# Twelve of sixteen gate projections by seven block products in a pass ahead of the attention, and the attention's fill laid out anew

## The chip, the core and the metric

The kernel runs on one core of one Trainium2 chip. The metric is the device time of one execution in microseconds (us); the kernel before takes 2233.44 us (median of three runs, 2233.07 to 2233.78). All arithmetic is on float32 values. Where the text says that a product is "split", each operand is written as a high part (a cast to the float32r type) plus a low part (the operand minus its high part), and three matmuls stand in place of one: high by high, low by high, high by low.

## The reference

One decoder layer on 1024 tokens of width 1024: a half feed-forward network, two attentions side by side that gates mix, a second half feed-forward network, and a gated embedding. What the change touches is the gate projections, in this middle part:

```python
h = rms_norm(x, mix_norm[i])
fq, fk, fv, f_logit, sq, sk, sv, g_fox, g_sb = split_columns(h @ w_in[i])
log_f = jax.nn.log_sigmoid((f_logit + forget_bias[i]).astype(jnp.float32))
y_fox = forgetting_attention(fq, fk, fv, log_f)      # 8 heads of 64
y_sb = stick_breaking_attention(sq, sk, sv)          # 8 heads of 64
merged = (jax.nn.sigmoid(g_fox) * (y_fox @ w_branch_fox[i])
          + jax.nn.sigmoid(g_sb) * (y_sb @ w_branch_sb[i]))
x = x + merged @ w_out[i]
```

`g_fox` and `g_sb` are 1024 columns each. Together they are 2048 columns of `h @ w_in`, which the kernel makes in sixteen blocks of 128 columns, called gates 0 to 15 here (0 to 7 for fox, 8 to 15 for stick-breaking).

## The kernel before, in words

The layer is worked in this order: the first feed-forward network (`ffn`, with `products` and the loop over `seqn`, then the down projection), the opening of the mixer (`mix_start`, its `end`), the attention with a fill of projections (`attention`), the branch and output projections, the second feed-forward network, and the gated embedding. Within the feed-forward networks the order of all instructions is the order of the code (`tc.manual_schedule`); in the attention the Tile framework places them, with ties set by `order`.

Names that the text uses:

- `hT[half][b]` holds h, transposed (feature by token), for tokens 0 to 511 and 512 to 1023, as high (b = 0) and low (b = 1) part.
- **A plain gate** is made by `g_units` (L901): a weight block of 1024 by 128 is loaded into a RAW buffer (`fetch` or `wload`), `wsplit` makes its high part with a cast on ACT (L136) and its low part with two subtractions on POOL (L146), and for each half of the tokens `feat_steps` (L759) issues 24 matmuls of 128x512 (L763): 3 split terms by 8 blocks of the contraction. The result goes to the array `gd` in HBM, for gates 0 to 7 as it is by a copy on DVE (L914), for gates 8 to 15 after a Sigmoid on ACT (L916). Where gates 0 to 7 are used, `gated` (L1311) loads them and applies the Sigmoid then (L1313).
- **The seven block products** are used in the feed-forward networks alone. A pair of 128-column weight blocks, two halves of the contraction and two halves of the tokens make a 2 by 2 by 2 block product; eight block products are replaced by seven over sums and differences of weight blocks (`sums`, L459, on POOL, and `prep`, L469, which casts on ACT and subtracts on DVE, L112 and L113) and of blocks of h (the `combo_` helpers, L558 to L599, made once). One block product is 12 matmuls of 128x512 (L496). `evict` (L508) joins the products that share a result.
- **The attention** (L1135) goes head by head, h = 0 to 7 fox, 8 to 15 stick-breaking ("sb"). A head has four steps c = 0 to 3, each with two blocks of 128 queries, i = 2c and 2c + 1, against the (i + 1) * 128 keys so far. `scores` (L968) makes the logits on PE (L990, L991) and then works on them: fox on DVE (L995), Exp on ACT (L1001), POOL (L1003); sb with two Sigmoids on ACT (L998, L999), running products on DVE (scans, L966), POOL (L1013, L1017). `apply` (L1027) does the step before: transposes on PE (L1042), a cast on ACT (L1044), a subtraction on DVE (L1045), then the products with v on PE (L1065), summed on ACT and DVE (L1084, L1085).
- **The fill.** In between, `take` (L1244) issues projection matmuls that the attention needs later or that only have to be done somewhere: one twenty-second of what `fill[h]` holds at each of 22 calls in a head, 7 of them in step 0, 4 in step 1, 5 in step 2 and 6 in step 3. `fill[h]` consists of units: half a gate (24 matmuls of 128x512), a quarter of an sb head's q and k projection, or an eighth of a 256-column projection for the fox heads or for v. All sixteen gates were spread over the fill and the stretch ahead of head 0.
- `forget_logs` (L921) and `forget_sums` (L946) make the cumulated forget gates: 27 small operations on DVE with an Exp on ACT, and 30 small matmuls.
- Buffers rotate by tag (`slot`), and PSUM banks by tag (`bank`: "sc" 3, "pt" 2, "av" 1, "pf" 2). An instruction waits until the old use of its buffer is over. SP issues all DMAs, in one queue, in order.

## Time and profile before

| what | before |
|---|---|
| time, median of 3 runs | 2233.44 us (2233.07 to 2233.78) |
| span of the profiled execution | 2230.9 us |
| granted TensorE clock, mean | 1.000 |
| PE busy | 2218.2 us (99%), 10857 matmuls |
| DVE busy | 1490.2 us (67%) |
| ACT busy | 972.1 us (44%) |
| POOL busy | 813.9 us (36%) |
| first attention step (head 0) starts | 725.5 us |
| head 8, the first sb head, starts | 1022.3 us |
| head 15 starts | 1314.8 us |

The span runs from the first to the last instruction of one profiled execution. The runs' list of times does not say which of them was profiled, so the span stands for the execution's own time; it lies 2.5 us under the median of the times. A matmul's end is modelled and matmuls overlap, so PE counts as busy wherever matmuls follow each other closely. The places of the heads come from the first small score matmul of each head. Matmul records match LDWEIGHTS records one to one here.

### The profile page before, as it was taken

How to read it: one execution, taken by the hardware profiler on the slowest of the kernel's cores; microseconds unless marked ns; L12 is line 12 of the kernel's file. 1: busy time of each engine (PE TensorE's matmuls, PEld its weight loads, DVE VectorE, ACT ScalarE, POOL GpSimd, SP SyncE). 2: the span in 40 equal slices, each digit the busy share in tenths (PEclk: the TensorE clock that was granted, in tenths of full speed). 3: DMA queues.
4: the chain of work that ended last, by engine and by line, in shares of the span. 5: the costliest groups of instructions: out<-in, count | busy, mean ns of one | idle time of the engine just before them, and what ended most of it. 6: DMA issues, size and time to landing. Idle time of an engine off the chain costs nothing.

```text
span 2230.9 us, 29212 instructions
## 1 busy us (share of the span) xinstructions
PE 2218.2 (99%) x10857; PEld 1864.3 (84%) x10857; DVE 1490.2 (67%) x2188; ACT 972.1 (44%) x1694; POOL 813.9 (36%) x709
## 2 busy tenths in 40 slices
PE   9999999999999999999999999999999999999999
PEld 7888888888889888888988888887888888888887
DVE  7855545497895565666666676799654555778873
ACT  6433333333454555555456564245333333434441
POOL 0344444310015466455456654400644443200111
PEclk9999999999999999999999999999999999999999
DMA  8232322474433133132124236731423232655132
GB/s 325 94 121 84 112 101 98 152 291 149 147 132 96 29 95 95 29 98 69 39 72 118 62 125 215 266 140 55 140 95 118 85 128 81 254 199 208 62 119 89
DMA packets 187710, 278.03 MB, mean 125 GB/s; under 512 B 27944, under 2 KB 110120, under 8 KB 187568
## 3 DMA queue, kind: packets, MB, share of 16 engines
q1 hardware_dynamic: 187568, 276.17, 36.7%
q8 instruction: 85, 1.39, 0.3%
q14 instruction: 57, 0.47, 0.1%
HBM read 192.47 MB, written 75.27 MB: 120 GB/s over the span
## 4 chain that ended last, share of the span: by engine, by line
PE 91%; DVE 4%; ACT 2%; issue 1%; DMA 1%; POOL 0%; SPq 0%; DVEq 0%; ACTq 0%; POOLq 0%
PE ps L496 36%; PE ps L388 19%; PE ps L763 11%; PE ps L755 7%; PE ps L1307 4%; PE ps L1662 4%; PE ps L1065 3%; PE ps L1042 2%; PE ps L449 2%; PE ps L991 1%; PE ps L990 1%; PE ps L1357 1%; DVE H L113 1%; ACT H L112 1%; ACT T L1001 0%
## 5 line engine op out<-in xcount | busy, mean ns | idle before, releaser
L388 PE MATMUL ps<-H,H 128*128 128x512 f32 x2184 | 497.3, 389 | 0.0
L388 PEld LDWEIGHTS ps<-H,H 128*128 128x128 f32 x2184 | 409.5, 188 | 85.0
L496 PE MATMUL ps<-H,WL 128*128 128x512 f32 x1008 | 238.9, 389 | 0.0
L496 PEld LDWEIGHTS ps<-H,WL 128*128 128x128 f32 x1008 | 189.2, 188 | 39.3
L763 PE MATMUL ps<-H,WH 128*128 128x512 f32 x640 | 176.1, 401 | 0.0
L1045 DVE TENSOR_TENSOR PT<-ps,PT 128x512 fp32r<-128x512 f32 (+1 forms) x160 | 100.6, 634 | 78.5 <-ACT PT L1044 77.6
L496 PE MATMUL ps<-H,Q 128*128 128x512 f32 x576 | 137.4, 389 | 0.0
L396 DVE SCALAR_TENSOR_TENSOR X<-ps,X 128x512 f32<-128x512 f32 x168 | 108.6, 682 | 41.8 <-PE ps L388 41.7
L763 PEld LDWEIGHTS ps<-H,WH 128*128 128x128 f32 x640 | 113.5, 188 | 18.4
L496 PEld LDWEIGHTS ps<-H,Q 128*128 128x128 f32 x576 | 108.1, 188 | 22.5
L1044 ACT CAST PT<-ps 128x512 fp32r<-128x512 f32 (+1 forms) x160 | 86.9, 549 | 85.0 <-PE ps L1042 81.1
L146 POOL TENSOR_TENSOR WL<-RAW,WH 128x512 fp32r<-128x512 f32 (+1 forms) x92 | 108.6, 1202 | 39.4 <-ACT WH L136 28.0
L496 PE MATMUL ps<-X,WL 128*128 128x512 f32 x480 | 115.6, 390 | 0.0
L209 POOL TENSOR_TENSOR PT<-PT,RN 128x1024 f32<-128x1024 f32 x2 | 4.8, 2413 | 295.0 <-ACT RN L203 295.0
L1065 PEld LDWEIGHTS ps<-PT,X 128*128 128x128 f32 x640 | 96.7, 189 | 18.9 <-DVE PT L1045 4.7
L755 PE MATMUL ps<-WH,H 128*128 128x256 f32 (+2 forms) x576 | 111.4, 323 | 0.2 <-DVE log_f L818 0.2
L1065 PE MATMUL ps<-PT,X 128*128 128x256 f32 (+1 forms) x640 | 105.7, 283 | 2.7 <-DVE PT L1045 1.4
L496 PEld LDWEIGHTS ps<-X,WL 128*128 128x128 f32 x480 | 89.9, 188 | 19.1 <-DVE WL L113 0.5
L1003 POOL TENSOR_TENSOR T<-T,l 128x128 f32<-128x128 f32 (+3 forms) x64 | 73.2, 1150 | 88.9 <-DVE l L1002 83.6
L496 PE MATMUL ps<-H,PT 128*128 128x512 f32 x432 | 103.2, 390 | 0.2 <-DVE PT L113 0.2
L283 POOL TENSOR_TENSOR PT<-GF,RN 128x512 f32<-128x512 f32 x20 | 33.2, 1658 | 174.1 <-DVE GF L539 89.9
L496 PEld LDWEIGHTS ps<-H,PT 128*128 128x128 f32 x432 | 80.8, 188 | 18.0 <-DVE PT L113 1.3
(418 smaller groups left out, 4810.8 us busy)
## 6 DMA issues: line engine op xcount, KB each, us to landing
hidden<-PT SPq DMA_DIRECT2D x40, 512.0 KB, 3.1
WH<-in_ffn_w_gate_dram SPq DMA_DIRECT2D x38, 512.0 KB, 5.4
Q<-hidden SPq DMA_DIRECT2D x24, 512.0 KB, 6.4
hidden<-RN SPq DMA_DIRECT2D x22, 512.0 KB, 2.6
KH<-in_ffn_w_up_dram SPq DMA_DIRECT2D x20, 512.0 KB, 6.2
KL<-in_ffn_w_up_dram SPq DMA_DIRECT2D x20, 512.0 KB, 6.9
T<-in_ffn_w_down_dram SPq DMA_DIRECT2D x20, 512.0 KB, 4.4
RAW<-in_w_in_dram SPq DMA_DIRECT2D x18, 512.0 KB, 4.3
```

The lines of the kernel that those rows point to most:

```text
L146: ins = eng_lo.tensor_sub(lo[part], raw[part], f(hi[part]))
L388: pe(nc.tensor.matmul(groups[g][t][:], wt[:, b, k, t * P:(t + 1) * P], act[:, a, k, :], start=(fresh and n == 0), stop=(i in (6, 1, 4) and ...
L396: nc.vector.scalar_tensor_tensor(xs, groups[g][t][:], scale, xs, ALU.mult, ALU.add)
L496: pe(nc.tensor.matmul(ps[:], hl[:, a, k, :], rhs(m, b, k), start=(first and i == 0), stop=(final and i == 11), skip_group_check=True))
L755: pe(nc.tensor.matmul(ps[:, :n], hT[t // 4][a][:, k, (t % 4) * P:(t % 4 + 1) * P], w[k // d][b][:, k % d, :n], start=(i == 0), stop=(i == ...
L763: pe(nc.tensor.matmul(ps[:], w[a][:, k, :], hT[half][b][:, k, :], start=(i == 0), stop=(i == 23)))
L1003: nc.gpsimd.tensor_mul(T[:, :n], T[:, :n], l[:].broadcast_to([P, n]))
L1044: high = nc.scalar.copy(pt[:, 0, :width], ps[:, :width])
L1045: low = nc.vector.tensor_sub(pt[:, 1, :width], ps[:, :width], f(pt[:, 0, :width]))
L1065: pe(nc.tensor.matmul(o, lh, r, start=(kpair == c and i == 0), stop=(kpair == 0 and i == 3)))
L1307: pe(nc.tensor.matmul(ps[:], w[a][:, k, :], yT[g][b][:, k, half * 512:half * 512 + 512], start=(i == 0), stop=(i == 11)))
L1662: pe(nc.tensor.matmul(ps, pl["w"][d, k // 2][b][:, k % 2, m * P:(m + 1) * P], hT[half][a][:, k, cs], start=(i == 0), stop=(i == 23)))
```

## The change

- Gates 0 to 11 leave the fill. `gate_pass`, called at the end of the mixer's opening, makes them in six pairs (`NG = 6`) by seven block products each: 504 matmuls of 128x512 instead of 576. Sums of weight blocks are made on POOL, low parts of weights on DVE; the sums and differences of h are made once, in eighteen DVE operations of 128x1024 (sixteen of them ahead of the first product) and eight ACT casts, from the tiles that the norm left (which are kept: the tags of `last_norms` and `second_half` change).
- The units that were run ahead of the attention (`u1[4:]` and `u2[4:]`, four eighths each of v and of q and k for heads 0 and 1) now run at the start of the pass, between those operations. `forget_logs` comes in the middle of them, `forget_sums` after the thirteenth product.
- The Sigmoid of all gates is applied where they are made; `gated` no longer applies it.
- Gates 12, 13 and 14 stay in the fill of fox heads 2, 4 and 6, and gate 15 in that of heads 12 and 13. `fill` is laid out anew: every head but head 5 holds less, and v for sb heads 12 to 15 is spread over heads 8 to 11.

```diff
+NG = 6
...
-            side = second_half(N[1], (38, 80, 15), lambda: bank("pt"), lambda: bank("pt"), ("PT", "PT", "PT", "Q"))
+            side = second_half(N[1], (38, 80, 15), lambda: bank("pt"), lambda: bank("pt"), ("PT", "PT", "KH", "KH"))
...
+            gate_pass(N)
...
+    def gate_pass(N):
...
+        seqn = [(0, 1), (0, 2), (1, 1), (1, 2), (0, 5), (1, 5), (0, 6), (1, 6), (0, 7), (1, 7), (0, 3), (0, 4), (1, 3), (1, 4), (2, 1), (2, 2), (2, 6), (2, 5), (2, 7)]
...
+        seqn += [(n, 1), (n - 1, 4), (n, 6), (n, 5), (n, 7), (n, 4), (n - 1, 3), (n, 2), (n, 3)]
...
+        def prep(n, m):
+            tag = ("WL", "WL", "WL", "WH", "WH", "WH")[turn_[0] % 6]
...
+            split(hl[:, 0], hl[:, 1], part(n, m), nc.scalar, nc.vector)
+            if m == 1:
+                sums(n)
...
+        def t1(i):
...
+            nc.vector.tensor_sub(c[:], wa(i)[:], c[:])
+            nc.scalar.copy(pair(5, 0, i), c[:])
...
+        def t23(i):
+            nc.vector.tensor_sub(wa(i)[:], wb(i)[:], wa(i)[:])
+            nc.vector.tensor_sub(wb(i)[:], wb(i)[:], C[i][:])
...
+        units = [g for _, g in mx["u1"][4:] + mx["u2"][4:]]
+        load(0)
+        prep(0, 1)
+        t1(0)
+        t1(1)
+        run(units[0])
+        load(1)
+        l1(0)
+        l1(1)
+        run(units[1])
+        prep(0, 2)
+        t23(0)
+        t23(1)
+        run(units[2])
+        prep(1, 1)
+        s(0, 6, wb)
+        run(units[3])
+        mx["sums"] = forget_logs(slot("WH", [P, 6, NT * NH]))
+        s(0, 7, wa)
+        run(units[4])
...
+        run(units[7])
+        s(1, 6, wb)
+        s(1, 7, wa)
+        t4(1)
...
+        for q, (n, m) in enumerate(seqn):
+            evict(n, m, product(n, m))
+            if q == 1:
+                s(0, 4, wa)
+                s(1, 4, wa)
+            for x in seqn[q:q + LA + 1]:
...
+                    prep(*x)
+            if q == 12:
+                forget_sums(mx["sums"])
...
+        fetch(c1w[0], c1w[1])
+        place(c1w[0], c1w[1])
+        fetch(c1w[2])
+        place(c1w[2])
+        fetch(c1w[3])
+        place(c1w[3])
         fs = fst(0)
-        run_all([fs[0], g0[0], fs[1]])
...
+        run_all([fs[0], c1[0], fs[1], c1[1]])
...
+        fill = [c1[2:5], c1[5:], ga + uq[:2], uq[2:], gb + c2[:3], c2[3:], gc, u8]
+        u9, uv = sst(9), v_units(SV + 256, 0, vs1)
+        fill.append(u9 + uv[:2])
+        fill.append(sst(10) + uv[2:4])
+        fill.append(sst(11) + uv[4:6])
+        fill.append(uv[6:] + sst(12))
...
+        fill.append(u + gs_[:n])
+        fill.append(sst(14) + gs_[n:2 * n])
+        fill.append(sst(15) + gs_[2 * n:])
         fox_branch = fox_branch_units()
-        fill.append(g15[1:] + fox_branch[:8])
+        fill.append(fox_branch[:8])
...
         nc.sync.dma_start(dst, gd[gate * KD + m, :, half * 512:half * 512 + 512])
-        order("act", nc.scalar.activation(dst, dst, AF.Sigmoid))
```

How the change moves instructions shows at three places. In each, a row is one instruction of the engine, result `<-` operands, and its width.

DVE at the end of the mixer's opening, first before: after the last statistics of q and k (qkss) come the low part of v (X) and a copy of the forget logits for one unit after the other, each from the bank (ps) that PE has filled.

```order
L849 TENSOR_SCALAR qkss_5018<-qkss_5018 128x16
L113 TENSOR_TENSOR X_4867<-ps_5160,X_4867 128x4x64
L818 COPY log_f<-ps_5160 128x8
L113 TENSOR_TENSOR X_4867<-ps_5188,X_4867 128x4x64
L818 COPY log_f<-ps_5188 128x8
L113 TENSOR_TENSOR X_4867<-ps_5216,X_4867 128x4x64
```

The same place in the changed kernel, where WL is a weight block's split, and Q, PT and KH are blocks of h:

```order
L850 TENSOR_SCALAR qkss_5018<-qkss_5018 128x16
L114 TENSOR_TENSOR WL_5156<-KL_5152,WL_5156 128x512
L1242 TENSOR_TENSOR Q_4760<-PT_4990,Q_4760 128x1024
L1242 TENSOR_TENSOR Q_4763<-PT_5009,Q_4763 128x1024
L114 TENSOR_TENSOR X_4867<-ps_5168,X_4867 128x4x64
L819 COPY log_f<-ps_5168 128x8
L1246 TENSOR_TENSOR X_5163<-Q_4760,X_5163 128x1024
L1246 TENSOR_TENSOR X_5163<-Q_4763,X_5163 128x1024
L114 TENSOR_TENSOR X_4867<-ps_5202,X_4867 128x4x64
L819 COPY log_f<-ps_5202 128x8
L114 TENSOR_TENSOR WL_5230<-KL_5153,WL_5230 128x512
L1249 TENSOR_TENSOR PT_4990<-KH_5037,PT_4990 128x1024
```

Between one unit's two DVE operations and the next unit's now stand two to five operations for the pass.

PE in the last step of head 12 (an sb head), first before: scores of the block of 1024 keys (L990, L991), fill (L763), transposes of the step before (L1042), fill.

```order
L990 MATMUL ps_11025<-KH_10297,Q_10296 128x512
L991 MATMUL ps_11025<-KL_10298,Q_10296 128x512
L990 MATMUL ps_11030<-KH_10297,Q_10296 128x512
L991 MATMUL ps_11030<-KL_10298,Q_10296 128x512
L763 MATMUL ps_10961<-H_4398,WL_10711 128x512 x3
L763 MATMUL ps_11042<-H_4396,WH_10866 128x512 x3
L1042 MATMUL ps_11055<-identf,T_10903 128x128
L1042 MATMUL ps_11055<-identf,T_10927 128x128 x2
L763 MATMUL ps_11042<-H_4396,WH_10866 128x512 x5
```

The same place in the changed kernel:

```order
L991 MATMUL ps_11306<-KH_10784,Q_10783 128x512
L992 MATMUL ps_11306<-KL_10785,Q_10783 128x512
L991 MATMUL ps_11311<-KH_10784,Q_10783 128x512
L992 MATMUL ps_11311<-KL_10785,Q_10783 128x512
L764 MATMUL ps_11255<-H_4397,WH_11030 128x512 x3
L1043 MATMUL ps_11321<-identf,T_11185 128x128
L1043 MATMUL ps_11321<-identf,T_11208 128x128 x2
L764 MATMUL ps_11255<-H_4397,WH_11030 128x512 x4
```

The pieces of fill are 3 and 4 matmuls where they were 6 and 5. Counted over steps 2 and 3 of this head, the fill is 36 matmuls where it was 59.

ACT in head 2 (a fox head), first before: casts of fetched weights (L136), the sum of an output block (L1084), then the Exps of two blocks (L1001) and a cast of transposed weights of the attention (L1044).

```order
L136 CAST WH_6424<-RAW_6327 128x1024
L136 CAST WH_6429<-RAW_6330 128x1024
L1084 COPY Y_5575<-ps_6355 64x256
L1001 ACTIVATE T_6453,l_6455<-T_6453,m_6454 128x384
L1001 ACTIVATE T_6470,l_6472<-T_6470,m_6471 128x512
L1044 CAST PT_6491<-ps_6487 128x384
```

The same place in the changed kernel, where the fill of this head holds gate 12:

```order
L137 CAST WH_7209<-RAW_7089 128x1024
L137 CAST WH_7214<-RAW_7092 128x1024
L1085 COPY Y_6404<-ps_7115 64x256
L917 ACT_TABLE_LOAD
L917 ACTIVATE PT_7206<-ps_7095 128x512
L1002 ACT_TABLE_LOAD
L1002 ACTIVATE T_7193,l_7195<-T_7193,m_7194 128x384
L1002 ACTIVATE T_7223,l_7225<-T_7223,m_7224 128x512
L1045 CAST PT_7243<-ps_7239 128x384
```

A Sigmoid (L917) now stands ahead of the Exps, with a load of ACT's function tables before it and another behind it. Over the whole kernel there are 19 such loads where there were 5; 12 of the added 14 stand in heads 2, 4 and 6.

More of the change, by code (lines that the diff above doesn't have):

```diff
@@ L602, in ffn, with last_norms @@
         nxt = []
[L604 removed]
+        def last_norms(i, t, own, tags_=(("PT", "RN", "GF", "RN"), ("GF", "RN", "KH", "KL"), tail.get("h", ("PT", "PT", "KH", "KL")))):
             if i == 0:
@@ new lines, in attention @@
+        c2[0] = at(c2[0], (place, c2w[3:]))
+        c2[5] = at(c2[5], (fetch, [gcw]))
+        c2[6] = at(c2[6], (place, [gcw]))
+        u8 = sst(8)
+        gc[1] = at(gc[1], (weights, (stacks[8], 1)))
+        fill = [c1[2:5], c1[5:], ga + uq[:2], uq[2:], gb + c2[:3], c2[3:], gc, u8]
[4 more added lines that the diff above has]
+        fill.append(uv[6:] + sst(12))
+        u, gs_ = sst(13), [g_units(m) for m in range(2 * NG + 3, 2 * KD)]
```

180 lines of the change are left out of this document (121 added, 59 removed).

## The prediction

> **What bounds the kernel now.** I read the page first: busy times, then the chain of work that ended last, by engine.
>
> ```profile
> span 2230.9 us, 29212 instructions
> PE 2218.2 (99%) x10857; PEld 1864.3 (84%) x10857; DVE 1490.2 (67%) x2188; ACT 972.1 (44%) x1694; POOL 813.9 (36%) x709
> PE 91%; DVE 4%; ACT 2%; issue 1%; DMA 1%; POOL 0%; SPq 0%; DVEq 0%; ACTq 0%; POOLq 0%
> ```
>
> PE is busy for 99% of the span and carries 91% of the chain. As long as that holds, time goes down only with PE's work. The same chain in order of time has one long piece, in the first feed-forward network, which is made of seven block products:
>
> ```profile
> 62.24 389.12 PE ps L496 x1716
> ```
>
> 389.12 / 1716 = 0.2268 us from one 512-wide matmul to the next, and no wait in 389 us. This is the price of a matmul below. It also shows that the product scheme, with its preparations and evictions, can stay behind PE once it runs.
>
> The 99% are a mean. What the change makes thin is the attention, so I asked for windows: the two halves of an sb head (head 11: steps 0 and 1, then 2 and 3), the second half of head 14, and fox head 6. Columns: window, length, then busy us and instructions of PE, PEld, DVE, ACT, POOL, then PE's clock, DMA share and GB/s.
>
> ```profile
> 1150.50:1170.40 19.90, 19.90 (x109) 16.93 (x109) 9.40 (x18) 9.82 (x21) 7.24 (x11) 1.00 0.19 57
> 1170.40:1191.30 20.90, 20.90 (x114) 17.98 (x114) 17.27 (x21) 13.25 (x28) 15.61 (x16) 1.00 0.34 89
> 1293.50:1314.80 21.30, 20.95 (x113) 17.66 (x112) 17.94 (x23) 15.19 (x31) 12.93 (x16) 1.00 0.42 134
> 952.40:990.40 38.00, 37.31 (x210) 31.40 (x209) 24.80 (x73) 22.27 (x43) 24.42 (x24) 1.00 0.42 112
> ```
>
> In head 11 DVE has 9.40 us of work in the first half and 17.27 in the second, where PE has 20.90. So PE has only 3.6 us more than DVE there: fill is what keeps PE busy while DVE makes the running products and low parts. This is the point on which the change turns.
>
> **What it removes.** 576 matmuls become 504: 72 x 0.2268 = 16.3 us. PE has no idle share to speak of, so all of it would come off the span if nothing else came late. The forget sums move behind the thirteenth product, and with that goes the wait in front of L956:
>
> ```profile
> L956 PE MATMUL ps<-GF,log_f 128*8 128x128 f32 x16 | 3.0, 272 | 1.1 <-DVE log_f L939 1.1
> L956 PEld LDWEIGHTS ps<-GF,log_f 128*8 128x8 f32 x16 | 1.4, 89 | 1.5 <-issue 1.2
> ```
>
> 1.1 us by the matmuls' group, 1.2 by the weight loads'. I take -1.2. What is late there next is the pass's own opening.
>
> **What it adds: the opening of the pass.** Up to the sixth product, PE has the units that it had before (some 23.5 us of the 24.00 in the first row below) and five products of 12 matmuls (60 x 0.2268 = 13.6): 37.1 us. DVE has in that time what it had, and the new blocks of h and of weights. The rows: DVE in the window of before, a 128x1024 subtraction of the same kind in the first network, the low part of a weight block, the old units' own subtraction, and the sum of a bank:
>
> ```profile
> 685.00:709.00 24.00, 24.00 (x202) 23.93 (x200) 10.63 (x30) 8.90 (x19) 16.46 (x12) 1.00 0.26 68
> 685.00:713.00 28.00, 26.94 (x228) 26.28 (x227) 13.61 (x45) 10.14 (x22) 16.99 (x13) 1.00 0.29 76
> L576 DVE TENSOR_TENSOR GF<-Q,GF x2: 1217/1217/1217, 47.8 to 1524.4; 128x1024 f32<-128x1024 f32 x2
> L113 DVE TENSOR_TENSOR WL<-RAW,WL 128x512 fp32r<-128x512 f32 x44 | 41.5, 944 | 11.3 <-ACT WL L112 11.3
> L113 DVE TENSOR_TENSOR X<-ps,X 128x256 fp32r<-128x256 f32 x4 | 1.7, 424 | 9.2 <-ACT X L112 9.2
> L523 DVE TENSOR_TENSOR Y<-Y,ps 128x512 f32<-128x512 f32 x22 | 15.1, 685 | 23.6 <-PE ps L496 23.6
> ```
>
> DVE: 13.6 + 18 x 1.217 = 21.9 + six low parts 5.7 + one sum 0.7 = 41.9 us. DVE's queue is in order, and each projection unit's bank is emptied by an L113 and an L818 that now stand behind two to five of the new operations, so PE waits in small pieces for "ps" and for X, T, GF, and last for the low part of the sixth product. 41.9 - 37.1 = 4.8; I take +5. It is 0 if DVE starts early (ahead of the old units' four subtractions it sat idle for 9.2 us), and 9 if the drains of banks and DVE's total add up rather than overlap.
>
> **The pass once it runs.** A pair is 84 matmuls, 19.05 us of PE. DVE has seven low parts and three sums, 7 x 0.94 + 3 x 0.69 = 8.6 us; the long piece of 389 us above did the same. I cost it at nothing; PE's products hide it, and without that cover it would be up to 8.6 us a pair. The Sigmoids move from the tail to the pass. In the tail they were hidden under PE too, which was busy 53.0 of 53 us there, so nothing comes back:
>
> ```profile
> 1372.00:1425.00 53.00, 53.00 (x235) 43.88 (x235) 33.24 (x41) 9.13 (x14) 31.96 (x26) 1.00 0.70 244
> ```
>
> **The boundary between pass and attention.** The weights of c1 go into the WH buffers that the last products still read and, through RAW, wait for POOL. A cast, a low part in two subtractions, and a load:
>
> ```profile
> L136 ACT CAST WH<-RAW 128x1024 fp32r<-128x1024 f32 x3 | 3.1, 1057 | 1.1 <-PE ps L755 1.1
> L146 POOL TENSOR_TENSOR WL<-RAW,WH 128x512 fp32r<-128x512 f32 x6 | 7.6, 1296 | 3.4 <-ACT WH L136 3.4
> RAW<-in_w_in_dram SPq DMA_DIRECT2D x18, 512.0 KB, 4.3
> ```
>
> Counted from the end of the last product but one, 2.7 us before the pass ends: cast 1.06 + 2 x 1.30 + load 4.3 + the next cast 1.06 = 9.0, so 6.3 us after the end. PE has about 1.8 us of other work there. I take a wait of +4.5, between 0 (an earlier buffer is free) and 8 (the second subtractions count too). SP's queue is in order, so the loads behind that one wait as well. PE's clock is 1.00 in every window above, and the wait of 1.2 us at L956 is the longest PE wait I found in this stretch. The Trainium skill, "TensorE: Matmul & The Clock Gate", section "HAM oscillation — how this bites in real kernels", warns that PE should not stand idle for more than about 3.4 us, since the clock then halves until PE has been busy for such a stretch again; as an estimate from that page this would add some 1.7 us to a wait of 4.5. No run here shows it yet; the sum goes by the clock of the rows.
>
> **The thinner attention, sb heads 8 to 13.** Each loses fill in every step; over steps 2 and 3 of head 12 it is 36 matmuls for 59, so 23 x 0.2268 = 5.2 us. PE has then 20.9 - 5.2 = 15.7 us where DVE has 17.27: DVE is the later one by 1.6, and since its work waits in turn for Sigmoids and matmuls, it won't be gapless. I take 2.0 a head, 6 x 2.0 = +12. The lower end is 0, if DVE's lag runs over into the next head's first half, where DVE has slack (9.40 of 19.90). The upper end is 5.2, the whole saving, if the steps are paced by their chain of Sigmoid, scan, POOL and transposes and not by work at all; a row that speaks for that is DVE's scan of the same size, which takes 0.75 us in one place and 1.86 in another of the same head:
>
> ```profile
> 1165.22 0.75 DVE L966 TENSOR_TENSOR_SCAN RN<-GF,RN 128x255 f32<-128x255 f32 x1
> 1176.56 1.86 DVE L966 TENSOR_TENSOR_SCAN RN<-GF,RN 128x255 f32<-128x255 f32 x1
> ```
>
> **Head 14** loses 72 matmuls of its fill, half of them in steps 2 and 3: 36 x 0.2268 = 8.2. PE has 21.3 - 8.2 = 13.1 us against DVE's 17.94: +4.8, of which I take +4.5, between 1 (carried over into head 15) and 8.
>
> **The fox heads.** Gates 12 to 14 now bring a Sigmoid between the Exps of heads 2, 4 and 6, and with it 12 loads of function tables. One such load in the trace, and the instruction behind it:
>
> ```profile
> 700.28 1.28 ACT L929 ACT_TABLE_LOAD   x1
> 701.58 0.26 ACT L929 ACTIVATE KL<-KL 128x64 f32<-128x64 f32 x1
> ```
>
> 12 x 1.28 = 15.4 us of ACT, which is 22.27 of 38.00 us busy in head 6. ACT has room, but Exp and its sums stand in the chain from scores to transposes. I take a third on PE's path, 5.1, between 0 and all of it; heads 6 and 7 lose 48 and 24 matmuls, 10.9 and 5.4 us, and head 6 comes to 27.1 of 38.00, near DVE's 24.80: +1. Together +6 (0 to 15.4). The Trainium skill, "ScalarE: Activation LUTs", section "What ACT_TABLE_LOAD costs", gives 1283 ns for a load and about 1380 ns more for a drain at each switch of sets, 2.66 us. The trace agrees on the load; of the drain it shows nothing, as the next instruction starts 0.02 us behind it. By the page, 12 would be an estimated 31.9 us of ACT, a third of that 10.6, and the sum below 5.5 us higher; the row decides, and I stay with 5.1.
>
> **The sum.** -16.3 - 1.2 + 5 + 4.5 + 12 + 4.5 + 6 = +14.5 on the profiled span of 2230.9 gives 2245.4; the median of the runs lies 2.5 above that span, and with it the time is 2233.4 + 14.5 = 2248. About 0.2%, 4.5 us, is what a measurement of this kernel can tell from no change.
>
> **The rivals.** *The waits are carried over, and it is faster.* Over a whole sb head PE keeps more work than DVE: head 11 has 40.8 - 46 x 0.2268 = 30.4 us of PE, and 9.40 + 17.27 = 26.7 of DVE. If the next head's first half takes up the lag, the 12 become 0, head 14 about 3, opening and boundary 2 each, the tables little: -17.5 + 7.5 = -10, 2223. For it: DVE's slack in first halves. Against: queues are in order, and PE's transposes in step 3 and the next step 0 need just the results that are late. It decides if DVE's lag at the end of step 3 stays under the some 5 us that the next first half has spare.
>
> *Break-even.* Half of the attention's waits are hidden and the opening costs what I say: -17.5 + 5 + 4.5 + 6 + 2 + 3 = +3, near 2236, or a little under before.
>
> *The chain sets the pace, and it is much slower.* If the second half of an sb head stays at 20.9 us without its fill, the six heads cost 31.2 instead of 12, and with more of the table loads on the path (11 instead of 5) the sum is +14.5 + 19.2 + 6 = +40, 2273. For it: scans that take twice as long beside POOL, and pieces of fill of 3 and 4 matmuls (0.7 and 0.9 us) that cover less of a cast and a subtraction. Against: POOL and ACT are below PE in every window.
>
> *That the gates don't get cheaper* can be left out: the changed order has 72 matmuls less.
>
> **How the numbers follow.** Forecast 0.50, with a range of its own from 2239 to 2262; carried over 0.23; break-even 0.15; the chain 0.12. The range of 8 in 10 goes from 2220, which takes in the faster case with the opening fully hidden, to 2264; above it lie the chain's case and little of the forecast's upper bounds. Faster by over 0.2%: the rival's 0.23 and a part of break-even, 0.27. Within: 0.13. Slower: 0.60.
>
> **What would show it.** PE's matmuls fall by 72, and the piece of the pass reads 504 x 0.2268 = 114 us of PE with idle time at its start (small waits for DVE, about 5 us) and none in its middle. Between the last product and the first score stands one wait of 4 to 5 us for c1's weights. In heads 8 to 13 PE's idle time of 2 us each stands in steps 2 and 3 and is released by DVE (L1045, L966); DVE is then over 90% busy there. Head 14 shows the most. ACT's table loads are 19, and PE waits behind them in heads 2, 4 and 6. It is wrong if sb heads get shorter by the full 10.4 us (the first rival), or if they get shorter by less than 6 (the chain), or if the pass itself shows idle time throughout.

## The result, and the profile after

| | before | after |
|---|---|---|
| time, median | 2233.40 us (2233.07 to 2233.78) | 2316.70 us (2312.62 to 2318.59) |
| ratio, 95% interval | | 1.0371 (1.0356 to 1.0385) |
| span of the profiled execution | 2230.9 us | 2315.1 us |

The changed kernel is slower by 83 us, with 72 matmuls less. The page of the changed kernel, first lines and the shares of the chain:

```profile
span 2315.1 us, 29224 instructions
PE 2235.6 (97%) x10785; PEld 1865.7 (81%) x10785; DVE 1551.8 (67%) x2250; ACT 1016.5 (44%) x1764; POOL 820.7 (35%) x709
PE 39%; DVE 7%; ACT 2%; issue 2%; DMA 0%; POOL 0%; ACTq 0%; DVEq 0%; POOLq 0%
```

PE's count falls by 72 as forecast, but PE is "busy" for 17.4 us more. A part of that is the clock, which is at half speed in some stretches of the changed kernel (last section): four 256-wide matmuls (started at 711.0 us) count 1.05 us in one of them, and four of the same kind 0.64 us behind it (714.7). So PE's busy share can't tell where the time went; the lengths of the stages can. The windows of before, cut at the first score of head 0, of head 8 and of head 15:

```profile
1.30:725.50 724.20, 721.80 (x3386) 602.78 (x3387) 489.33 (x605) 294.32 (x464) 213.66 (x153) 1.00 0.42 147
725.50:1022.30 296.80, 293.87 (x1715) 254.44 (x1714) 179.75 (x564) 161.15 (x345) 165.03 (x167) 1.00 0.25 68
1022.30:1314.80 292.50, 291.91 (x1663) 253.80 (x1662) 192.78 (x280) 161.27 (x338) 163.70 (x181) 1.00 0.28 81
1314.80:2230.90 916.10, 910.60 (x4101) 753.31 (x4099) 628.01 (x738) 354.86 (x548) 270.85 (x203) 1.00 0.40 140
```

The same cuts in the changed kernel:

```profile
1.30:867.80 866.50, 844.65 (x3890) 700.65 (x3891) 555.15 (x684) 350.32 (x559) 249.04 (x176) 0.99 0.39 136
867.80:1164.40 296.60, 269.90 (x1546) 229.61 (x1545) 171.20 (x548) 175.37 (x358) 157.36 (x161) 0.97 0.21 57
1164.40:1401.50 237.10, 215.07 (x1278) 186.22 (x1277) 196.32 (x277) 145.67 (x319) 145.76 (x167) 0.98 0.24 67
1401.50:2315.10 913.60, 906.00 (x4076) 749.24 (x4075) 628.77 (x740) 344.61 (x529) 267.84 (x201) 1.00 0.40 139
```

The first column after the window is its length. Up to head 0 it grew by 142.3 us, for 504 matmuls (114.3 us). The eight fox heads have 169 matmuls less by the records, some 38 us, and **are in sum not shorter**: 296.8 before, 296.6 after (experiment 3 takes them one by one). Heads 8 to 14 lost about 87 us of PE's work and are 55.4 us shorter. The rest is 2.5 us shorter for 24 matmuls less. 142.3 - 0.2 - 55.4 - 2.5 = 84.2, the difference of the spans. What PE waits for in the changed kernel, first from 684 to 868 us (opening, pass and boundary), in total, times, longest:

```profile
PE ps L756 <- DVE log_f L819: 8.3, 3, 7.2
PE ps L756 <- ACT Y L137: 2.7, 1, 2.7
PE ps L756 <- ACT RN L846: 2.3, 1, 2.3
PE ps L1195 <- DVE G L1209: 2.0, 1, 2.0
PE ps L756 <- ACT WH L137: 2.0, 1, 2.0
PE ps L957 <- POOL WL L951: 1.5, 1, 1.5
PE ps L1195 <- DVE WH L114: 1.5, 1, 1.5
```

Then in the fox heads, first before, 725.5 to 1022.3:

```profile
PE ps L1065 <- DVE PT L1045: 0.8, 4, 0.2
PE ps L1065 <- ACT PT L1044: 0.6, 1, 0.6
PE ps L882 <- DVE Y L1085: 0.5, 1, 0.5
PE ps L990 <- DVE m L995: 0.3, 1, 0.3
```

And after, 867.8 to 1164.4:

```profile
PE ps L1066 <- ACT PT L1045: 8.8, 9, 2.1
PE ps L1066 <- DVE PT L1046: 5.8, 9, 1.3
PE ps L1066 <- DVE KL L871: 3.4, 6, 1.1
PE ps L883 <- POOL RN L853: 2.5, 2, 1.9
PE ps L1043 <- POOL T L1004: 2.2, 1, 2.2
PE ps L992 <- DMA KL<-KL: 1.4, 1, 1.4
PE ps L883 <- DVE Y L1086: 0.9, 2, 0.5
```

And from there to head 15, again first before (1022.3 to 1314.8), then after:

```profile
PE ps L1065 <- DVE PT L1045: 0.6, 2, 0.3
```

```profile
PE ps L1066 <- DVE PT L1046: 21.1, 19, 1.8
```

In the sb heads PE waits for DVE alone; in the fox heads for ACT, DVE, POOL and a DMA in turn. This difference turns out to matter. The two halves of head 11 after, to be held against those of before:

```profile
1267.60:1283.00 15.40, 15.01 (x113) 14.21 (x112) 10.61 (x18) 9.47 (x22) 9.33 (x11) 1.00 0.17 35
1283.00:1301.30 18.30, 15.94 (x88) 13.08 (x87) 17.86 (x23) 11.95 (x26) 14.29 (x16) 1.00 0.21 44
```

In the second half DVE is busy for 17.86 of 18.30 us. That part of the forecast, 17.27 us of DVE's work as the pace, came as it was worked out.

### The profile page after: what moved, and what is told of

It reads as the page before. It is cut to its first block, busy times and chain, and to the rows that moved or that the text cites. A ratio compares the mean times of both kernels' runs of the same rounds, so it can differ in the third digit from the quotient of the medians.

```text
span 2315.1 us, 29224 instructions
## 1 busy us (share of the span) xinstructions
PE 2235.6 (97%) x10785; PEld 1865.7 (81%) x10785; DVE 1551.8 (67%) x2250; ACT 1016.5 (44%) x1764; POOL 820.7 (35%) x709
## 4 chain that ended last, share of the span: by engine, by line
PE 39%; DVE 7%; ACT 2%; issue 2%; DMA 0%; POOL 0%; ACTq 0%; DVEq 0%; POOLq 0%
PE ps L497 17%; PE ps L389 8%; PE ps L1813 4%; PE ps L1459 3%; DVE RN L967 3%; PE ps L764 2%; PE ps L1066 2%; DVE PT L1046 1%; PE ps L1043 1%; PE ps L450 1%; DVE H L114 1%; ACT T L1000 0%; ACT H L113 0%; ACT GF L999 0%; PE ps L992 0%
## 5 line engine op out<-in xcount | busy, mean ns | idle before, releaser
L1066 PE MATMUL ps<-PT,X 128*128 128x256 f32 (+1 forms) x640 | 120.2, 296 | 43.6 <-DVE PT L1046 28.9
L1004 POOL TENSOR_TENSOR T<-T,l 128x128 f32<-128x128 f32 (+3 forms) x64 | 73.3, 1149 | 105.2 <-DVE l L1003 104.6
L967 DVE TENSOR_TENSOR_SCAN RN<-GF,RN 128x127 f32<-128x127 f32 (+2 forms) x96 | 95.7, 997 | 2.8
L147 POOL TENSOR_TENSOR WL<-RAW,WH 128x512 fp32r<-128x512 f32 (+1 forms) x70 | 80.5, 1170 | 46.1 <-ACT WH L137 27.7
L756 PEld LDWEIGHTS ps<-WH,H 128*128 128x128 f32 x576 | 87.0, 194 | 10.5 <-ACT WH L137 2.4
## 6 DMA issues: line engine op xcount, KB each, us to landing
X<-in_x_dram SPq DMA_DIRECT2D x16, 512.0 KB, 10.2
```

The lines of the kernel that those rows point to most:

```text
L147: ins = eng_lo.tensor_sub(lo[part], raw[part], f(hi[part]))
L756: pe(nc.tensor.matmul(ps[:, :n], hT[t // 4][a][:, k, (t % 4) * P:(t % 4 + 1) * P], w[k // d][b][:, k % d, :n], start=(i == 0), stop=(i == ...
L967: order("dve", nc.vector.tensor_tensor_scan(*args))
L1004: nc.gpsimd.tensor_mul(T[:, :n], T[:, :n], l[:].broadcast_to([P, n]))
L1066: pe(nc.tensor.matmul(o, lh, r, start=(kpair == c and i == 0), stop=(kpair == 0 and i == 3)))
```

## The experiments

Except where the text says otherwise each is an edit of the changed kernel, with one timed execution, beside one of the kernel before on the same chip (2233.2 to 2233.9). The changed kernel's own runs spread over 6 us, so the times are read together with the lengths of stages in the trace.

**1. Is fill what the heads lack?** Matmuls that nothing reads, put into the fill (`dummy` multiplies blocks of `hT` into a bank of its own):

```diff
+        for x, k in ((0, 1), (1, 1), (2, 1), (3, 1), (4, 1), (6, 2), (7, 1)):
+            fill[x] = fill[x][:1] + [(24 * 0.216, dummy(24, "pf")) for _ in range(k)] + fill[x][1:]
```

> The changed kernel with 192 more matmuls of 128x512, 43.5 us of PE's work, in the fill of fox heads 0 to 4, 6 and 7 (24 each, 48 in head 6), the amount that the change took out of them; they use only h, and nothing reads their results. Theory 1, the fox heads' waits stand there because fill no longer covers a chain that takes its time: two thirds of the matmuls are free, and the time is 2328 to 2338. Theory 2, the waits come from the table loads and from where things were moved: at least 36 us more, 2352 or above.

Measured: 2328.6 us, 11.9 more for 43.5 us of work. The fox heads in that run:

```profile
869.00:1175.50 306.50, 301.25 (x1738) 260.72 (x1737) 171.65 (x548) 176.93 (x358) 157.50 (x161) 0.99 0.20 55
```

306.5 us with 192 matmuls more, where it was 296.6: 33.6 of the 43.5 us were free, more than the two thirds that theory 1 asked for. Up to some 6 us of that may be the clock: one stretch of half clock falls into these heads here, and five did in the changed kernel (the last section prices one at up to 1.5 us). The waits in the list above fall from 25 us to 4.5:

```profile
PE ps L1072 <- ACT PT L1051: 2.5, 3, 1.7
PE ps L1072 <- DVE PT L1052: 1.1, 4, 0.4
PE ps L889 <- DVE Y L1092: 0.5, 2, 0.3
PE ps L997 <- DMA KH<-KH: 0.4, 1, 0.4
```

The free share is not the same in each head. Heads 0 and 1 grew by 2.2 and 4.8 us, back to the 32.6 and 36.3 us of before: of their 10.9 us of matmuls 7.0 had to be paid for. Heads 2, 3, 4, 6 and 7 took 32.7 us of matmuls for 2.9. There, fill that is taken out buys little. The same for heads 8 to 14, with 48 matmuls each and 72 in head 14:

```diff
+        for x in range(8, 15):
+            fill[x] = fill[x][:1] + [(24 * 0.216, dummy(24, "pf")) for _ in range(2 + (x == 14))] + fill[x][1:]
```

> The changed kernel with 360 more matmuls of 128x512, 81.7 us of PE's work, in the fill of heads 8 to 14 (48 each, 72 in head 14), near the amount that the change took out of them; they use only h, and nothing reads their results. Theory, DVE sets these heads' pace and the matmuls fill PE's waits: about 30 of the 81.7 us are free, 2363 to 2373. Rival, the waits there are not such that fill can stand in them: less than 12 free, 2386 or above.

Measured: 2375.0 us, 58.3 more; the heads went from 237.1 to 295.9 us:

```profile
1163.00:1458.90 295.90, 288.76 (x1639) 249.88 (x1638) 184.11 (x277) 149.82 (x320) 139.51 (x167) 1.00 0.20 54
```

22.9 us of 81.7 were free here: between theory and rival, nearer to the theory. Of the matmuls put into the sb heads some 28% were free, of those put into the fox heads 77%.

**2. What sets the sb heads' pace?** The subtraction on DVE behind each group of transposes left out in sb heads, the matmuls reading the high part twice (so the low part of the weights is missing from the result):

```diff
-                for b in range(2):
+                for b in ((0, 1) if step["fox"] else (0, 0)):
...
+            if step["fox"]:
+                nc.vector.tensor_sub(pt[:, 1, :width], ps[:, :width], f(pt[:, 0, :width]))
```

> The changed kernel, but in the sb heads the low part of the transposed weights is left out (no subtraction on DVE; the matmuls read the high part twice), so DVE has about 6 us less in each of heads 8 to 15 and PE the same matmuls. Theory 1, DVE's work sets the pace of steps 2 and 3: heads 8 to 13 go from 34 to about 30.5 us, head 14 from 33 to 29, some 25 us off in all, about 2292. Theory 2, the chain from Sigmoid through scan and POOL to the transposes sets it: heads stay above 33, less than 8 us off in all.

Measured: 2303.8 us, 12.9 less, half of what theory 1 gave. Heads 8 to 13 together, and the second half of head 11:

```profile
1164.30:1350.50 186.20, 180.62 (x1131) 160.22 (x1130) 143.08 (x182) 123.61 (x274) 136.45 (x142) 1.00 0.24 62
1274.10:1289.80 15.70, 15.26 (x88) 13.02 (x87) 15.19 (x18) 12.12 (x26) 13.85 (x15) 1.00 0.26 55
```

Heads 8 to 13 take 186.2 us where they took 204.1: 31.0 each for 34.0, as theory 1 said to within 0.5. In the second half of head 11, with the same 88 matmuls, DVE has 2.7 us less work (15.19 for 17.86), and the half is 2.6 us shorter. Head 14 moved by 1.2 only, and the stretch behind it got 6 us longer, where PE now waits 4.7 us for the split of the attention's result (L114 on DVE), so the time fell by less. The length of heads 8 to 13 follows DVE's work; that of head 14 does not. The edit also takes a link out of the way from the transposes to the products with v, so that way has to be tried by itself.

If it were this way that lacks cover, the products could simply come later:

```diff
-        turn_and_scan(c)
-        for kpair in range(c - 1, -1, -1):
+        for kpair in range(c, -1, -1):
             turn_and_scan(kpair)
-            values(kpair + 1)
+            if kpair + 2 <= c:
+                values(kpair + 2)
...
+        if c:
+            values(1)
```

> The changed kernel, but in the attention the products with v come two groups of transposes behind their own, not one, so that a cast and a subtraction have one more piece of fill and one more group to be done in; no work is added. Theory 1, the waits at these products (some 38 us in all heads) are the time from transposes through cast and subtraction that thin fill no longer covers: 15 to 30 us off, 2287 to 2302. Theory 2, DVE's work in sb heads and Exp with its table loads in fox heads set the pace: less than 6 us off.

Measured: 2318.1 us. Theory 1 falls. The waits moved from the products to the transposes behind them, which now wait for the bank that DVE's subtraction has to free (L1043 here is the transposes, "<- DVE" their bank's last reader):

```profile
PE ps L1066 <- DVE PT L1046: 23.3, 26, 1.8
PE ps L1043 <- DVE PT L1046: 15.9, 16, 2.7
```

So heads 8 to 13 go by DVE's work and not by the length of this way.

**3. The fox heads: table loads, and which chain.** ACT in head 2 of the changed kernel, in order of time (start, length):

```profile
941.88 1.28 ACT L917 ACT_TABLE_LOAD   x1
943.17 0.60 ACT L917 ACTIVATE PT<-ps 128x512 f32<-128x512 f32 x1
943.79 1.28 ACT L1002 ACT_TABLE_LOAD   x1
945.09 0.62 ACT L1002 ACTIVATE T<-T,m 128x384 f32<-128x384 f32 x1
```

A gate's eviction is 3.2 us of ACT where a copy on DVE was 0.7. Gates 12 to 14 stored by a copy:

```diff
-            if m < KD:
+            if m < 2 * NG + 3:
                 nc.vector.tensor_copy(g[:], ps[:])
...
+        if 2 * NG <= gate * KD + m < 2 * NG + 3:
+            order("act", nc.scalar.activation(dst, dst, AF.Sigmoid))
```

> The changed kernel, but gates 12, 13 and 14 are stored without their Sigmoid, by a copy on DVE, and get it in the tail, as in the kernel before. Theory 1, the table loads between the Exps are what heads 2, 4 and 6 lose: these heads, 39.7, 49.5 and 36.6 us long, fall to 102 to 106 in sum, and the time to about 2296. Theory 2, the fill is too thin there for a chain that was just as long before: the heads stay within 5 us of their sum of 125.8, and the time is 2311 or more.

In the kernel that ran these three gates got no Sigmoid at all: they belong to stick-breaking, whose branch doesn't use `gated`. Measured: 2304.3 us; heads 2, 4 and 6 take 114.3 us for 125.8. That is between the two theories: the six Sigmoids with their 12 loads, and with the half clock that comes with their waits (below), cost 11.5 us, almost a us for each load, and the rest of what the fox heads lost is something else. With the gates exchanged, the pass making gates 4 to 15 and the fill 0 to 3 with their Sigmoid in the tail, so that all is computed:

```diff
-            c0 = GFOX + n * 256
+            c0 = GFOX + 512 + n * 256
...
+        if m < 4:
+            order("act", nc.scalar.activation(dst, dst, AF.Sigmoid))
         nc.vector.tensor_mul(dst, dst, ps[:])
```

> The changed kernel with the pass over gates 4 to 15, and gates 0 to 3 in the fill, stored by a copy and with the Sigmoid in the tail as in the kernel before: all of the computation, and no table load between the Exps. As where the Sigmoid of three gates was left out: heads 2, 4 and 6 fall from 125.8 to about 114, and the time to 2302 to 2306. If the eight Sigmoids in the tail were on the path there, 2307 or more.

Measured: 2306.8 us, at the edge of what was expected; the fox heads take 282.4 us, 14.2 less, and the same three heads 113.7. The time fell by 10.0 from the profiled run's 2316.8, mainly since head 0 starts 3.6 us later. The fox heads:

```profile
871.40:1153.80 282.40, 263.90 (x1546) 225.47 (x1545) 174.29 (x554) 156.64 (x340) 157.61 (x161) 0.99 0.22 60
```

The other way round, in the kernel before, with thick fill and no other part of the change: `g_units` applies the Sigmoid to all gates, `gated` doesn't.

```diff
-            if m < KD:
-                nc.vector.tensor_copy(g[:], ps[:])
-            else:
-                order("act", nc.scalar.activation(g[:], ps[:], AF.Sigmoid))
+            order("act", nc.scalar.activation(g[:], ps[:], AF.Sigmoid))
```

> The kernel before, with the Sigmoid of gates 0 to 7 moved to where they are made, as in the changed kernel, and no other part of the change: the added table loads come under the old, thick fill. Theory 1, a table load costs what it is wherever it stands between Exps: some 8 us more for the three or four fox heads that get one, 2241 to 2250. Theory 2, thick fill hides them: within 4 us of 2233.

Measured: 2243.8 us, 10.4 more than before, with 25 table loads for 5: half a us for each, of 1.28. So thick fill hides a part of them, and not the same part everywhere: head 6, with seven loads and one stretch of half clock, is 7.3 us longer, heads 2 and 3 with four and three 1.2 and 2.3, and head 4 with three only 0.2. Experiment 1 agrees: there heads 2, 4 and 6 have as much of PE's work as before and the loads, and are 4.4 us longer than before in sum.

Head by head the lengths are as follows. The heads start at their first small score matmul; PE's work is its matmuls' columns at 0.2268 us for 512. The last two columns are experiment 1 and the run with the gates exchanged.

| head | PE's work, change | before | after | fill put back | no Sigmoid between the Exps |
|---|---|---|---|---|---|
| 0 | -5.4 | 32.6 | 30.4 | 32.6 | 30.4 |
| 1 | -5.4 | 36.3 | 31.5 | 36.3 | 31.4 |
| 2 | -5.4 | 37.5 | 39.7 | 41.4 | 34.9 |
| 3 | -5.4 | 36.7 | 36.1 | 37.1 | 34.5 |
| 4 | -5.4 | 47.5 | 49.5 | 47.9 | 44.3 |
| 5 | +5.4 | 36.3 | 42.0 | 42.0 | 42.0 |
| 6 | -10.9 | 38.0 | 36.6 | 38.1 | 34.5 |
| 7 | -5.4 | 31.8 | 30.8 | 31.1 | 30.3 |

So "not shorter" is a sum of unlike parts. Head 5 got more fill and grew by as much: it follows PE. Head 1 gave back 4.8 of its 5.4 us. Heads 2, 4 and 6 lost 21.8 us of PE's work and grew by 2.8; without the Sigmoids between the Exps they would still have given back 9.3 only.

What else sets their length? The low part left out in fox heads instead of sb heads:

```diff
-                for b in range(2):
+                for b in ((0, 0) if step["fox"] else (0, 1)):
...
+            if not step["fox"]:
+                low = nc.vector.tensor_sub(pt[:, 1, :width], ps[:, :width], f(pt[:, 0, :width]))
```

> The changed kernel, but in the fox heads the low part of the transposed weights is left out (no subtraction on DVE; the matmuls read the high part twice): about 6 us less of DVE in each of heads 0 to 7 and a shorter way from transposes to the products with v, PE's matmuls the same. Theory 1, that way sets the fox heads' length where fill is thin: their sum of 296.7 us falls by 10 or more, 2306 or less. Theory 2, it is set ahead of it, from scores through maximum, Exp, reciprocal and POOL to the transposes, with the table loads in it: at most 4 us off.

Measured: 2312.4 us; the fox heads take 288.9 us, 7.7 less, between the two again, though DVE lost a quarter of its work there:

```profile
869.50:1158.40 288.90, 266.49 (x1546) 229.79 (x1545) 125.55 (x472) 175.75 (x358) 157.79 (x161) 0.97 0.21 58
```

The heads got about 1 us shorter on average (0.3 to 2.4). No engine is busy for more than 61% here besides PE. This fits a chain through several engines, each waiting for the one before; it isn't shown link by link, and which link is the longest stays open.

**4. The pass's own 28 us.** First, low parts of weights that wait for a buffer of the units moved behind these units:

```diff
-        prep(0, 2)
         t23(0)
...
-        prep(1, 1)
         s(0, 6, wb)
         run(units[3])
+        prep(0, 2)
+        prep(1, 1)
```

> The changed kernel, but in the opening of the pass the low parts for products (0,2) and (1,1) come behind the fourth unit, whose weights hold the buffers that they wait for, not ahead of the third and fourth. Theory 1, the long PE wait there (7.2 us, and the half clock after it) comes from ACT's and DVE's queues standing behind that buffer: the wait goes, no half clock there, 10 to 13 us off, about 2304. Theory 2, DVE simply has too much work in the opening (41.9 us of it against 37.1 of PE): the wait moves to the next place, and at most 4 us go.

Measured: 2314.2 us. The waits of 7.2 and 2.3 us became 3.7 and 4.7; head 0 starts when it did, 866.7 us after the first matmul for 866.5. Theory 2 holds: the wait moved to the next place. Eight of the operations on POOL:

```diff
-            nc.vector.tensor_sub(wa(i)[:], wb(i)[:], wa(i)[:])
-            nc.vector.tensor_sub(wb(i)[:], wb(i)[:], C[i][:])
+            nc.gpsimd.tensor_sub(wa(i)[:], wb(i)[:], wa(i)[:])
+            nc.gpsimd.tensor_sub(wb(i)[:], wb(i)[:], C[i][:])
...
-            nc.vector.tensor_sub(wa(i)[:], f(hi), wb(i)[:])
-            nc.vector.tensor_add(wa(i)[:], wa(i)[:], f(lo))
+            nc.gpsimd.tensor_sub(wa(i)[:], f(hi), wb(i)[:])
+            nc.gpsimd.tensor_add(wa(i)[:], wa(i)[:], f(lo))
```

> The changed kernel, but eight of the sixteen subtractions and sums of h's blocks ahead of the first product are on POOL, not on DVE (9.7 us less of DVE there). Theory 1, DVE's amount of work sets the opening: 6 to 9 us off, about 2309. Theory 2, the opening is a chain of results in which each engine waits for the one before, and POOL takes twice as long for the same operation: no gain, up to 6 us slower.

Measured: 2326.1 us, slower by 9 (by 15 up to head 0), more than either theory allowed. One of these operations took 2.34 to 3.23 us on POOL where it took 1.21 to 2.20 on DVE, and PE's longest wait is now 9.6 us, for a cast on ACT. And fourteen operations left out, so that products read blocks of h that are not theirs:

```diff
-            t = B[m]
+            t = B[5]
...
-        t23(0)
-        t23(1)
...
-        t4(0)
...
-        s(1, 6, wb)
-        s(1, 7, wa)
-        t4(1)
```

> The changed kernel without fourteen of the eighteen 128x1024 operations on h's blocks and six of their eight ACT casts; the products that would read these blocks read the two that are left (same matmuls, other data). 17.0 us less of DVE's work in the opening. Theory 1, the amount of DVE's and ACT's work there makes PE wait (7.4, 2.4 and 1.6 us, and the half clock): 12 us off or more, 2304 or less. Theory 2, the units' buffers, loads and the forget logs set the opening: at most 5 us off.

Measured: 2304.2 us. But of these 12.5 us only 6.7 are in the stage, which takes 859.8 us for 866.5. The others stand in heads that the edit doesn't touch: 3.1 in heads 2 and 3, where a stretch of half clock is gone (below), the rest mostly in heads 4 and 6, with no cause shown. The opening in the changed kernel, and here up to the same product:

```profile
685.00:741.00 56.00, 43.87 (x276) 39.81 (x275) 43.22 (x74) 20.71 (x36) 25.75 (x12) 0.91 0.04 10
```

```profile
685.00:733.00 48.00, 42.09 (x273) 38.77 (x273) 23.39 (x59) 15.81 (x32) 21.76 (x12) 0.96 0.04 12
```

DVE has 43.2 us of work in the opening, as worked out (41.9), and the opening takes 56, not 43. PE has about 38 us of work in it (the forecast's 37.1 and four matmuls), so it loses some 18. With 20 us of DVE's work gone it takes 48. So the amount of DVE's and ACT's work is somewhat under half of the opening's loss. The rest is not shown; I argue that it lies in the order, in which DVE, ACT and PE wait for one another in turn. Next, the loads behind the pass made earlier (the pairs' buffers exchanged, `fetch` and `place` of c1's weights among the last seven products):

```diff
-            W[n] = {"r": [slot(("KL", "RAW")[n % 2], [P, 4, 256]) for _ in range(2)], "left": 7}
+            W[n] = {"r": [slot(("RAW", "KL")[n % 2], [P, 4, 256]) for _ in range(2)], "left": 7}
...
+            if q == len(seqn) - 7:
+                fetch(c1w[0], c1w[1])
+            if q == len(seqn) - 5:
+                place(c1w[0])
+                fetch(c1w[2])
+            if q == len(seqn) - 4:
+                place(c1w[1])
+                fetch(c1w[3])
+            if q == len(seqn) - 2:
+                place(c1w[2])
...
```

> The changed kernel, but the weights of c1 come earlier: the last pair of gates is held in KL, so that RAW comes free seven products before the end of the pass, the first two loads are issued there, and the casts go to the buffers that come free first. Theory 1, the two waits after the pass (2.1 and 3.0 us) and the 6.8 us of half clock that starts behind the first of them are all due to these loads: 6 to 9 us off, about 2309. Theory 2, ACT's casts or POOL's low parts are late anyway: at most 3 us off.

Measured: 2317.1 us. The two waits by L137 went from 2.0 and 2.7 us to 0.9 and 2.7. Theory 1 falls; the early loads were not what was late. I argue, and haven't shown, that the last weights' buffer is: it is free only when two blocks before it have gone through ACT and POOL. Last, four pairs for six (gates 8 to 11 are not made):

```diff
-        last_n = NG - 1
+        last_n = 3
...
-            if W[n]["left"] == 0 and n + 2 < NG:
+            if W[n]["left"] == 0 and n + 2 < 4:
...
```

> The changed kernel with four pairs in the pass, not six (gates 8 to 11 are not computed; the results of four others are stored in their places, so that the stores stay the same): 168 matmuls of 128x512 less, 38.1 us, all in the pass. Theory 1, what the pass loses is its opening and its end, whatever its length: 2278 to 2282. Theory 2, each pair loses its share (28 us in six pairs): 2266 to 2272.

Measured: 2284.6 us, 32.1 off for 38.1 us of work. The pass does not get better with fewer pairs: its loss is 142.3 - 114.3 = 28 us with six and, with head 0 starting 111.5 us later than before for 336 matmuls (76.2 us), 35 with four. 4 us of the difference are longer waits at the boundary (6.3 and 2.6 us by L137 for 2.7 and 2.0), which I can't explain. The time lies above the range of either theory. Theory 1 is the nearer one: no part of the loss went with the two pairs.

**5. Does PE's half clock cost anything?** 56 matmuls that nothing reads, put where PE waits longest in the opening and behind the pass:

```diff
         s(0, 7, wa)
+        run(dummy(28))
         run(units[4])
...
+        run(dummy(8))
         run(units[7])
...
+        run(islice(c1[0][1], 4))
+        run(dummy(8))
+        run(islice(c1[0][1], 2))
+        run(dummy(12))
```

> The changed kernel with 56 more matmuls of 128x512 (12.7 us of PE's work, of h alone, nothing reads them) at the places where PE waits longest: 28 and 8 in the opening of the pass, 8 and 12 in the two waits behind it. Theory 1, the half clock behind these waits is on the path: more work, and yet 4 to 8 us less, about 2310. Theory 2, what sets the time there is DVE, ACT and the loads, and PE at half clock is quick enough: within 3 us of 2316. If the matmuls don't fit into the waits: up to 12 us more.

Measured: 2316.6 us, and head 0 starts at the same time (866.4 us). All 56 were free, 12.7 us of PE's work, but half clock came back at two other places in the stage (10.2 us in all, for 17.1), so theory 1 was not tested cleanly. What it shows is that PE has 12.7 us to spare in this stage. That DVE and ACT set the time there is argued from it.

## Why the prediction was wrong

Slower was right, and the size was not: 2248 forecast, range to 2264, 2316.7 measured. Its steps, as length of each stage:

| stage | forecast | measured |
|---|---|---|
| up to head 0 | +114.3 - 1.2 + 5 + 4.5 = +122.6 | +142.3 |
| fox heads, 38.1 us of fill less | -38.1 + 6 = -32 | -0.2 |
| heads 8 to 13, about 71 us less | -71 + 12 = -59 | -47.0 |
| head 14, 16.3 us less | -16.3 + 4.5 = -12 | -8.3 |
| head 15 and behind, 5.4 us less | -5 | -2.5 |

The forecast's column is its terms beside the matmuls that each stage gained or lost, rounded; it adds up to its +14.5. The measured column adds up to 84.3.

- **The step that failed is "Together +6", the fox heads.** It priced the table loads and heads 6 and 7, and took it that all other fill goes off the path, since PE was busy for 99% and "as long as that holds, time goes down only with PE's work". It never put the fox heads' own chain beside PE, as it did for the sb heads with DVE. The step gave the fox heads 6 us, 15.4 at most, beside 38.1 us of matmuls that were to come off; by the lengths it cost 37.9. The runs show two parts. The Sigmoids with their loads, and the half clock that comes with them, are 14.2 of it (the run with the gates exchanged), where 5.1 was taken. The other 24 us, for which the step had 1, are fill whose removal didn't shorten the heads: 33.6 of 43.5 us put back were free, most of it in heads 2, 3, 4, 6 and 7. In heads 1 and 5 the step's premise held, and they followed PE. No engine's busy share shows this (24.80 of 38.00 us of DVE in head 6 looked harmless). It is 32 of the 69 us that the forecast missed. Which chain holds these heads stays open.
- **The table loads** were taken at a third, 5.1 us. Without them heads 2, 4 and 6 were 11.5 and, with all gates computed, 12.1 us shorter. The upper bound of 15.4, all of the loads' time on the path, held this. The Trainium skill ("ScalarE: Activation LUTs", section "What ACT_TABLE_LOAD costs") speaks of 2.66 us for each switch with its drain; the trace shows 1.28, and the next instruction 0.01 and 0.02 us behind the two loads in the rows above, so it shows no drain behind a load.
- **The opening**, forecast +5, lost some 18 us, the second largest miss. DVE's 41.9 us were about right (43.2), the assumption that DVE and PE would each go through theirs in parallel was not. Waits of 7.2, 2.3 and 1.5 us stand there, and 10.2 us of half clock. The end of the range, 9, "if the drains of banks and DVE's total add up rather than overlap", was itself too low.
- **The boundary**, forecast +4.5: 4.7 us of waits by L137, as forecast; its cause is not the one named, since earlier loads changed little.
- **The pass once it runs**, forecast at nothing: waits of 2.0 us for a bank and 0.7 for a cast; nearly right. The -1.2 for `forget_sums` did not come: PE waits 1.5 us there, now for POOL (L957).
- **The clock** was taken at 1.00 by the windows of before, with a wait of 4.5 us as the one that might lower it. It was halved in ten stretches, 44 us in all, most of them behind 1.5 to 2.4 us of idle time. In head 3 a stretch costs 1.5 us; what they cost in all is not separated from the waits that they follow.
- **The sb heads**: the mechanism was right, DVE's second half. 2.0 a head was forecast; 24 us over six heads, 4.0 a head, came, within the 0 to 5.2 that it gave. The heads got 7.8 us shorter each, between the 6 and the 10.4 that would have spoken against it. The rival "carried over", with DVE's lag taken up by the next first half, didn't occur; DVE had 10.61 of 15.40 us there and still the time did not come back.
- **The rival "the chain sets the pace"**, at 0.12 and with an end of 2273, comes nearest. But it put the chain into the sb heads, where DVE's work was the pace, and of the fox heads it had only more of the table loads.

No version of the changed kernel here beats the kernel before. The pass loses 28 us where it saves 16.3, ahead of any loss in the attention.

## What to carry to other kernels

When work that fills waits is to be taken out, first ask how long the stage would be without it: by the busiest engine's work if one is near full, and by the dependent chain, which no busy share shows. Matmuls that nothing reads, put in, measure it: the share of their time that the stage doesn't grow by is time that PE had to spare. Ask it head by head, since a sum can hide stages that follow PE and stages that don't. A function on ACT that needs another table, put between others, cost about a us for each load of 1.28 us under thin fill and half a us under thick fill here, so it is neither free nor always on the path.

## What the hardware showed

**The clock falls after much shorter idle times than was cited.** In the kernel before, PE's clock is 1.00 throughout the stages. In the changed kernel it is halved in ten stretches of 3.4 us or a multiple, although the longest single wait outside the opening is about 2.7 us. They start on a fixed raster of 3.41 us: the first four at 702.6, 852.8, 965.4 and 989.3 us, which are 44, 33 and 7 periods of 3.413 us apart. Each follows a period of this raster in which PE idled for 1.5 us or more (1.54 to 2.36, worked out from the matmuls' starts and ends). It is no sharp limit: two periods with 1.7 and 1.8 us were not followed by one, and in experiment 5 a period with 1.3 was. Head 3 shows it: two periods of the changed kernel, then the same place in the run with the gates exchanged (experiment 3), whose raster lies otherwise.

```profile
985.90:989.30 3.40, 1.16 (x11) 0.93 (x10) 1.76 (x11) 0.92 (x2) 3.40 (x4) 1.00 0.00 0
989.30:992.70 3.40, 3.40 (x18) 3.40 (x17) 1.03 (x3) 2.06 (x5) 3.40 (x4) 0.50 0.03 5
```

```profile
983.60:987.00 3.40, 1.96 (x15) 1.72 (x13) 2.72 (x14) 0.94 (x3) 3.40 (x4) 1.00 0.00 0
987.00:990.40 3.40, 2.62 (x23) 2.62 (x24) 0.90 (x3) 2.09 (x6) 3.40 (x4) 1.00 0.00 0
```

In both PE waits 2.2 us for POOL (L1004). In the first the wait falls into one period (1.16 of 3.40 busy), and the next runs at 0.50. In the second it is cut by the raster (1.96 and 2.62 busy), and the clock stays. Head 3 takes 36.0 to 36.1 us in five of the runs in which such a stretch falls into it with nothing else changed there, and 34.5 to 34.6 us in six in which none does. So a wait costs up to 1.5 us more by the place of the raster. This would explain why the changed kernel's times spread over 6 us where the kernel before has 0.7, and why some heads moved that an experiment didn't touch; beyond heads 2 and 3 it is not shown. The Trainium skill, "TensorE: Matmul & The Clock Gate", section "HAM oscillation — how this bites in real kernels", warns of idle gaps above about 3.4 us: the length of the period agrees, the gap does not, as 1.5 to 2.2 us within a period are enough here.
